# Two fused pairs of weights in group 9, background work in that group's first half, five heads under way, and another order of the pairs in the first output group

## The chip, the cores and the metric

The kernel runs on one core of one Trainium2 chip. The metric is the device time of one execution in microseconds (us), the median of several runs. TensorE is PE below, VectorE DVE, ScalarE ACT, GpSimd POOL and SyncE SP; PEld is the weight load of PE.

## The reference

One layer of an encoder works on x of 256 rows and 4096 columns, everything in float32:

```python
xn = rms_norm(x, norm_g)
h = einsum('bsd,de->bse', xn, w_in)                # 4096 x 14336
c_val, c_glu, c_gate, q, k, v, a_gate = split(h)   # seven parts of 2048 columns
conv_out = conformer_conv(c_val, c_glu, ...) * silu(c_gate)
q, k = rms_norm(q), rms_norm(k)                    # by head: 16 heads of 128
attn_out = longnet_mixture(q, k, v, rel_bias) * silu(a_gate)
y = x + einsum('bse,ed->bsd', concatenate([conv_out, attn_out]), w_out)   # 4096 x 4096
```

`conformer_conv` multiplies the value by a sigmoid gate, convolves every channel with 31 taps, normalises over the 2048 channels (LN below) and applies swish. `longnet_mixture` gives each head three patterns of dilated attention windows, combined by their softmax denominators.

## The kernel before

**Groups and pairs.** The two projections are 18 groups of 1024 output columns. Groups 0 to 3 give the convolution's value and GLU gate, 4 and 5 its gate, 6, 7, 9 and 11 queries and keys of four heads each (qk0 to qk3), 8, 10, 12 and 13 value and gate of four heads each (agv0 to agv3), and 14 to 17 are the output projection. A group runs over 4096 rows of weights in 16 steps, its slots; what a slot works on is a *pair*: two blocks of 128 rows, 256 x 1024 weights, 1 MB, loaded by SP (L252) into one of three `raw` buffers. Pairs are numbered through by u = 16 x group + slot, so `raw152` belongs to slot 8 of group 9. The next load into a buffer is issued when the last step of the pair that held it has been written.

**Plain and fused pairs.** Each float32 operand is split into a high and a low part, so that a product takes three fast matmuls (high x high, high x low, low x high). A *plain* pair costs ACT two casts (L1131, `wh`), DVE one subtraction (L1137, `wl`), and PE 24 matmuls of 512 columns (L1325, L1327). A *fused* pair is taken as a 2 x 2 block product with seven multiplications in place of eight, so PE runs 21 matmuls (L1192 to L1194, L1296, L1298); its weights need sums first: three subtractions L1155, the sums L1163, L1175, L1176 and the subtraction L1174 on DVE, and four casts on ACT (L1154, L1170). Four of its sums (m1, m5, m6, m7) gather in four more PSUM banks and are added to the group's result after the group's last fused pair, in the next plain pair (`add_more`: one copy by ACT, L1359, the rest on DVE, for the output groups L1363 to L1381). `FUSED` names the pairs that are fused: seven in most of groups 1 to 8, none in 9 to 13, four in group 14, seven in 15 to 17. `ORDERS` is the order of the pairs within a group. In group 14 pairs 0 to 7 are the 16 heads' columns of `w_out`'s rows (two heads a pair), 8 to 15 the convolution's.

**Weights ahead.** PE, DVE and ACT each run their instructions in the order in which the program wrote them. `Stream.step` writes the making of weights a few steps ahead of PE's use of them, as far as buffers go: four `ws` tiles and up to four halves under the tag `c4`, which they share with convolution and gate tiles (`C4` in number).

**Background work.** Between the weights the program writes everything else, in lanes of generators to which `pump` gives time for each matmul written (`credit`): convolution taps, LN, gates, heads, and the splitting of the projection's input for the output groups. One tap is four multiply-adds on DVE (L628), or four products by ACT (L562) that are added to the sum by DVE (L619) where `state["taps"]` is true, and otherwise by a DMA that POOL issues with an addition (L581). `head_lane = Lane(4)` lets four heads be under way at once. A head makes its scores (`psc`, L802, a short run of float32 matmuls on PE between the weights), bias and softmax (L812 to L830), a turn through DRAM (DVE L836, POOL L454 to write and L461 to read back), the product with the values (`po`, L847, again on PE) and the sum L852. Scores and `po` use the second set of PSUM banks (`state["side"]`), which only slots 1 up to the group's first fused pair give them. `mix_split_gen` (L865 to L890) makes the high and low parts `mh` and `ml` (L880, L882) of gated convolution and attention columns, pair by pair in the order of `ORDERS[14]`, and for the pairs that any output group fuses the sums `ms` and `msp` (L377 to L390). A convolution block's columns are ready when `gated_gen` has multiplied them with the gate (L733), which it loads back by four POOL DMAs (`far_g`, L461), block after block. Other POOL DMAs of that place are the write and the reads of a head's turned weights (`turn_p..d`, `pr`) and those of an attention gate (`turn_ag..d`, `agv`).

Of the kernel before, what the change touches and what calls it, by code (L numbers as in the profile page):

```python
# [11 lines left out]
F32 = mybir.dt.float32  # L12
F32R = mybir.dt.float32r
# [4 lines left out]
P = 128  # L18
# [24 lines left out]
SETTLED = 3000  # L43

CP_MIN = 900
C4 = 16

X_LOAD = {0: 12, 1: 16, 3: 20, 5: 24, 6: 28}
X_SQUARE = {4: 4, 5: 0, 6: 8, 7: 12, 8: 16, 9: 20, 10: 24, 11: 28}
# [17 lines left out]
FUSED_IN = range(1, 9)  # L67
SUMS = (2, 4, 6, 8, 10, 12, 13)
FUSED = [SUMS if g in FUSED_IN else () for g in range(N_IN)]
FUSED[1], FUSED[2] = (6, 8, 12), SUMS[1:]  # L70
FUSED += [range(4)] + 3 * [range(7)]
ORDERS = N_IN * [range(16)]
ORDERS += [(8, 9, 10, 11, 12, 13, 14, 0, 15, 1, 4, 2, 5, 3, 6, 7)]
ORDERS += 3 * [(8, 9, 0, 10, 1, 11, 2, 12, 3, 13, 4, 14, 5, 6, 15, 7)]

W_SLOTS, W_MORE = 4, 4
# [61 lines left out]
def layer_kernel(  # L138
# [16 lines left out]
    state = {"side": "side", "taps": True, "held": 0}  # L155
    const = ctx.enter_context(tc.tile_pool(name="const", bufs=1))
    sb = ctx.enter_context(tc.tile_pool(name="sb", bufs=1))
    ps = ctx.enter_context(tc.tile_pool(name="ps", bufs=1, space=bass.MemoryType.PSUM))

    def t4(name):  # L160
        return sb.tile([P, 4, 256], F32, tag="c4", bufs=C4, name=name)

    def t2(name):
        return sb.tile([P, 512], F32, tag="t2", bufs=5, name=name)

    def h2(name):
        return t2(name).rearrange("p (a b) -> p a b", a=2)
# [201 lines left out]
    def block_sums(j, src_of, parts, out, name, small=False):  # L369


        a11, a21, a12, a22 = (by_block(src_of[2 * j + k])[:, s] for k in range(2) for s in range(2))
        t = t2(f"{name}_{j}")
        s1, s2, s3, s4 = (
            t[:, P * i : P * i + P].rearrange("p (a i) -> p a i", a=4) for i in range(4)
        )
        nc.vector.tensor_sub(s1, a21, a22)  # L377
        nc.vector.tensor_sub(s2, s1, a11)
        yield 580
        nc.vector.tensor_sub(s3, a11, a21)  # L380
        nc.vector.tensor_add(s4, a12, s2)
        yield 580
        if small:
            both = [sb.tile([P, 512], F32R, tag="toep", bufs=4, name=f"{name}p{j}{i}") for i in "hl"]
        else:
            both = sb.tile([P, 2, 512], F32R, tag="c4", bufs=C4, name=f"{name}p{j}")
            both = both[:, 0], both[:, 1]
        nc.scalar.copy(both[0], t)
        yield 0, 620
        nc.vector.tensor_sub(both[1], t, both[0].bitcast(F32))  # L390
        names = {f"s{i + 1}": [b[:, P * i : P * i + P] for b in both] for i in range(4)}
        names["a11"] = [m[2 * j][:, :P] for m in parts]
        names["a12"] = [m[2 * j + 1][:, :P] for m in parts]
        names["a22"] = [m[2 * j + 1][:, P:] for m in parts]
        out[j] = names
        yield 690
# [146 lines left out]
    taps, made = deque(), deque()  # L543
# [239 lines left out]
    def head_gen(hg, hh):  # L783
        h = 4 * hg + hh
        hs = slice(DH * hh, DH * hh + DH)
        while hg not in qk_ready:
            yield
        T = sb.tile([P, 512], F32, tag="toep", bufs=4, name=f"T{h}")
        nc.sync.dma_start(
            T[:, :384],  # L790
            bass.AP(
# [9 lines left out]
        for it in range(2):  # L801
# [7 lines left out]
        window = bass.AP(  # L809
            tensor=T.tensor, offset=T.offset + S - 1, ap=[T.ap[0], [P, 2], [-1, 256]]  # L810
        )
# [76 lines left out]
            elif j in FUSED[-1]:  # L888
                later.append(j)

    post_lane, head_lane, gate_lane, mix_lane = Lane(2, (0,)), Lane(4), Lane(1, ()), Lane(1)
    fetch_lane, ag_lane = Lane(1, (1,)), Lane(1, ())
    conv_lane, ln_lane, cp_lane = Lane(1, ()), Lane(1, (0,)), Lane(1, (1,))
    center_lane = Lane(1, (1,))
# [150 lines left out]
    class Stream:  # L1045
# [159 lines left out]
        def group(self, g):  # L1205
# [3 lines left out]
            last_group, into = g == NG - 1, groups[g][0] == "out"  # L1209
# [8 lines left out]
            firsts = [s for s, j in enumerate(ORDERS[g]) if j in FUSED[g]]  # L1218
            window = range(1, (firsts + [n_pairs - 3])[0])
            for slot, j in enumerate(ORDERS[g]):  # L1220
                u = g * n_pairs + slot
                state["side"] = tags[1] if slot in window and len(window) > 4 else None
                state["taps"] = not firsts
                if g == n_in - 1:
                    progress["in"] = 2 * slot
                self.more = W_MORE if firsts and slot + 2 >= firsts[0] else 0
# [287 lines left out]
```

## Time and profile before

| | |
|---|---|
| runs | 1561.62 us median of 3 (1560.17 to 1565.84) |
| profiled execution, its own time | 1561.59 us |
| its span | 1559.8 us |
| matmul records on PE | 6844 |
| group 9 (windows of the trace) | 759.52 to 850.02 us |
| group 13 | 1126.14 to 1220.73 us |
| group 14 | 1220.73 to 1308.59 us |

The span runs from the first to the last instruction recorded; the execution's own time has 1.79 us around it. A group's limits are the starts of its first matmul and of the next group's.

### The profile page before, as it was taken

The numbers are of one execution on the slowest core, as the hardware profiler recorded it, in microseconds if no ns is written. First come the engines' busy times: TensorE is split into PE (matmuls) and PEld (weight loads), VectorE is DVE, ScalarE is ACT, GpSimd is POOL, SyncE is SP. The second block draws the span as 40 slices with busy tenths as digits, with TensorE's granted clock in tenths as the row PEclk, the third lists the DMA queues.
The fourth block names the chain that finished last, engine by engine and source line by source line (L and its number), as shares of the span: only waits on it lengthen the run. The fifth ranks groups of instructions, "written<-read, shape, count | busy, mean of one in ns | idle before, by whom it ended". The sixth has DMA issues, their size and how long they took to land.

```text
span 1559.8 us, 18654 instructions
## 1 busy us (share of the span) xinstructions
PE 1554.2 (100%) x6844; PEld 1285.2 (82%) x6844; DVE 1350.8 (87%) x1449; ACT 1017.3 (65%) x1564; POOL 148.5 (10%) x222
## 2 busy tenths in 40 slices
PE   9999999999999999999999999999999999999998
PEld 8888888888888888888888888888888888888887
DVE  7898799989899888999897989886676798998988
ACT  7665556767676677677778887776657654555453
POOL 0000000101010100001120012010240200000000
PEclk9999999999999999999999999999999999999999
DMA  9556567969788887789695668665886866666663
GB/s 350 199 201 231 189 218 241 274 218 267 241 258 254 243 246 256 228 247 251 226 313 188 230 229 266 213 230 203 251 270 209 252 223 230 239 217 240 234 240 119
DMA packets 80828, 367.91 MB, mean 236 GB/s; under 512 B 9152, under 2 KB 31296, under 8 KB 44128
## 3 DMA queue, kind: packets, MB, share of 16 engines
q1 hardware_dynamic: 50336, 317.86, 57.9%
q0 software_dynamic: 30112, 48.58, 14.3%
q8 instruction: 53, 0.87, 0.2%
q14 instruction: 39, 0.32, 0.1%
q10 hardware_dynamic: 288, 0.28, 0.1%
HBM read 328.57 MB, written 18.91 MB: 223 GB/s over the span
## 4 chain that ended last, share of the span: by engine, by line
PE 94%; DVE 2%; DMA 1%; issue 1%; ACT 1%; DVEq 0%; SPq 0%; ACTq 0%
PE c L1325 40%; PE c L1327 20%; PE m L1296 6%; PE c L1341 4%; PE m L1298 3%; PE c L1296 2%; PE c L1193 2%; PE c L1194 2%; PE c L1192 2%; PE c L1343 2%; PE acc L1033 2%; PE acc L1034 2%; PE acc L1036 2%; DMA raw<-in_w_dram 1%; PE c L1298 1%
## 5 line engine op out<-in xcount | busy, mean ns | idle before, releaser
L1137 DVE TENSOR_TENSOR wl<-raw,wh 128x2048 fp32r<-128x2048 f32 x196 | 448.2, 2289 | 146.9 <-ACT wh L1131 140.3
L1131 ACT CAST wh<-raw 128x1024 fp32r<-128x1024 f32 x392 | 390.7, 1047 | 194.0 <-PE c L1327 124.0
L1325 PE MATMUL c<-wh,nh 128*128 128x512 f32 x1152 | 450.2, 391 | 0.0
L1327 PE MATMUL c<-wh,nl 128*128 128x512 f32 x1152 | 448.4, 389 | 0.0
L1154 ACT CAST t<-raw 128x1024 fp32r<-128x1024 f32 x152 | 160.1, 1053 | 250.3 <-DVE raw L1163 171.1
L1325 PE MATMUL c<-wl,nh 128*128 128x512 f32 x1152 | 287.7, 392 | 0.0
L1325 PEld LDWEIGHTS c<-wh,nh 128*128 128x128 f32 x1152 | 216.3, 188 | 45.2
L1327 PEld LDWEIGHTS c<-wh,nl 128*128 128x128 f32 x1152 | 216.3, 188 | 45.1
L1325 PEld LDWEIGHTS c<-wl,nh 128*128 128x128 f32 x1152 | 216.3, 188 | 44.9
L1155 DVE TENSOR_TENSOR t<-raw,t 128x1024 fp32r<-128x1024 f32 x152 | 185.5, 1222 | 3.7 <-ACT t L1154 0.4
L562 ACT ACTIVATE cp<-a,wT 128x241 f32<-128x241 f32 (+14 forms) x312 | 131.4, 491 | 1.0 <-DVE cT L619 1.0
L1325 PE MATMUL c<-wh,mh 128*128 128x512 f32 x280 | 109.1, 390 | 0.0
L1327 PE MATMUL c<-wh,ml 128*128 128x512 f32 x280 | 108.9, 389 | 0.0
L581 POOL DMA_DIRECT2D cT<-cp x38 | 48.8, 1285 | 533.7 <-ACT cp L562 488.7
L1163 DVE TENSOR_TENSOR raw<-raw 128x1024 f32<-128x1024 f32 x76 | 93.1, 1225 | 2.6
L1155 DVE TENSOR_TENSOR b<-raw,b 128x1024 fp32r<-128x1024 f32 x76 | 92.7, 1220 | 1.6 <-ACT b L1154 1.0
L1154 ACT CAST b<-raw 128x1024 fp32r<-128x1024 f32 x76 | 79.6, 1047 | 3.5 <-PE c L1327 1.8
L1296 PE MATMUL m<-t,xsp 128*128 128x512 f32 x216 | 72.3, 389 | 0.0
L628 DVE SCALAR_TENSOR_TENSOR cT<-a,wT,cT 128x255 f32<-128x255 f32 (+8 forms) x168 | 68.9, 476 | 0.6
L1325 PE MATMUL c<-wl,mh 128*128 128x512 f32 x280 | 69.2, 389 | 0.0
L1327 PEld LDWEIGHTS c<-wh,ml 128*128 128x128 f32 x280 | 52.6, 188 | 10.9
L1325 PEld LDWEIGHTS c<-wl,mh 128*128 128x128 f32 x280 | 52.6, 188 | 10.9
(346 smaller groups left out, 2311.0 us busy)
## 6 DMA issues: line engine op xcount, KB each, us to landing
raw<-in_w_dram SPq DMA_DIRECT2D x286, 1024.0 KB, 5.0
xr<-in_x_dram SPq DMA_DIRECT2D x8, 512.0 KB, 6.5
out_dram<-xr SPq DMA_DIRECT2D x15, 256.0 KB, 7.5
xT<-in_x_cols_dram SPq DMA_DIRECT2D x7, 512.0 KB, 9.0
T<-bias_dram SPq DMA_DIRECT2D x16, 192.0 KB, 6.1
cT<-cp POOLq DMA_DIRECT2D x4, 488.0 KB, 6.7
cT<-cp POOLq DMA_DIRECT2D x4, 486.0 KB, 6.7
cT<-cp POOLq DMA_DIRECT2D x4, 484.0 KB, 6.1
```

Of the source, the lines that this page charges most:

```text
L562: nc.scalar.activation(cp[:, t, lo:hi], a[:, t, lo + sh : hi + sh], AF.Copy, scale=wT[:, 4 * cb + t, k : k + 1],)
L628: nc.vector.scalar_tensor_tensor(c[:, t, lo:hi], a[:, t, lo + sh : hi + sh], wT[:, 4 * cb + t, k : k + 1], c[:, t, lo:hi], op0=ALU.mult, o ...
L1131: nc.scalar.copy(h, raw_tiles[u][:, k])
L1137: nc.vector.tensor_sub(l, src, h.bitcast(F32))
L1154: nc.scalar.copy(h, src)
L1155: nc.vector.tensor_sub(l, src, h.bitcast(F32))
L1163: nc.vector.tensor_add(r[:, 0:4:3, :], r[:, 0:3:2, :], twice(r[:, 3, :]))
L1296: nc.tensor.matmul(acc, ah, b, start=begin, stop=end)
L1298: nc.tensor.matmul(acc, al, b, start=False, stop=False)
L1325: nc.tensor.matmul(acc, a[s][0], b[e], start=begin, stop=False)
L1327: nc.tensor.matmul(acc, a[s][1], b[e], start=False, stop=False)
L1341: nc.tensor.matmul(acc, a[s][0], b[e], start=False, stop=end)
```

## The change

The diff has five parts. `FUSED[9] = (8, 10)` makes the pairs in slots 8 and 10 of group 9 fused ones. `state["taps"]` says when DVE may add ACT's products; it was true in every slot of a group without fused pairs, and now also in slots 1 to 7 of group 9 (its `window`, up to the first fused pair), not after them. Scores, too, have their banks in that group in slots 1 to 7 only. `Lane(5)` lets a fifth head be under way, for which the turned weights `T` (tag `toep`) have five buffers instead of four and the tag `t2` six instead of five; `C4` gives up one tile for them. `ORDERS[14]` puts pairs 4 and 5 (heads 8 to 11) first, and its fused pairs 0 to 3 into slots 8, 10, 12 and 14, where they had slots 7, 9, 11 and 13; behind the last fused pair now stands one plain pair instead of two.

Counted over the whole program, the order has 6 matmuls of 512 columns fewer on PE, the two fused pairs' ones. The short runs of float32 matmuls (scores, `po` and LN's means) that stand between the weights' matmuls of groups 9 to 14 are 25 before and 17 after, with as many matmuls in them. DVE's tap multiply-adds (L628, four to a tap) go from 40 to 42 taps, its additions L619 from 40 to 37, and POOL's adding DMAs L581 from 38 to 39.

```diff
@@ -43,7 +43,7 @@
 SETTLED = 3000
 
 CP_MIN = 900
-C4 = 16
+C4 = 15
 
 X_LOAD = {0: 12, 1: 16, 3: 20, 5: 24, 6: 28}
 X_SQUARE = {4: 4, 5: 0, 6: 8, 7: 12, 8: 16, 9: 20, 10: 24, 11: 28}
@@ -67,10 +67,10 @@
 FUSED_IN = range(1, 9)
 SUMS = (2, 4, 6, 8, 10, 12, 13)
 FUSED = [SUMS if g in FUSED_IN else () for g in range(N_IN)]
-FUSED[1], FUSED[2] = (6, 8, 12), SUMS[1:]
+FUSED[1], FUSED[2], FUSED[9] = (6, 8, 12), SUMS[1:], (8, 10)
 FUSED += [range(4)] + 3 * [range(7)]
 ORDERS = N_IN * [range(16)]
-ORDERS += [(8, 9, 10, 11, 12, 13, 14, 0, 15, 1, 4, 2, 5, 3, 6, 7)]
+ORDERS += [(4, 5, 8, 9, 10, 11, 12, 13, 0, 14, 1, 15, 2, 6, 3, 7)]
 ORDERS += 3 * [(8, 9, 0, 10, 1, 11, 2, 12, 3, 13, 4, 14, 5, 6, 15, 7)]
 
 W_SLOTS, W_MORE = 4, 4
@@ -161,7 +161,7 @@
         return sb.tile([P, 4, 256], F32, tag="c4", bufs=C4, name=name)
 
     def t2(name):
-        return sb.tile([P, 512], F32, tag="t2", bufs=5, name=name)
+        return sb.tile([P, 512], F32, tag="t2", bufs=6, name=name)
 
     def h2(name):
         return t2(name).rearrange("p (a b) -> p a b", a=2)
@@ -381,7 +381,7 @@
         nc.vector.tensor_add(s4, a12, s2)
         yield 580
         if small:
-            both = [sb.tile([P, 512], F32R, tag="toep", bufs=4, name=f"{name}p{j}{i}") for i in "hl"]
+            both = [sb.tile([P, 512], F32R, tag="toep", bufs=5, name=f"{name}p{j}{i}") for i in "hl"]
         else:
             both = sb.tile([P, 2, 512], F32R, tag="c4", bufs=C4, name=f"{name}p{j}")
             both = both[:, 0], both[:, 1]
@@ -785,7 +785,7 @@
         hs = slice(DH * hh, DH * hh + DH)
         while hg not in qk_ready:
             yield
-        T = sb.tile([P, 512], F32, tag="toep", bufs=4, name=f"T{h}")
+        T = sb.tile([P, 512], F32, tag="toep", bufs=5, name=f"T{h}")
         nc.sync.dma_start(
             T[:, :384],
             bass.AP(
@@ -888,7 +888,7 @@
             elif j in FUSED[-1]:
                 later.append(j)
 
-    post_lane, head_lane, gate_lane, mix_lane = Lane(2, (0,)), Lane(4), Lane(1, ()), Lane(1)
+    post_lane, head_lane, gate_lane, mix_lane = Lane(2, (0,)), Lane(5), Lane(1, ()), Lane(1)
     fetch_lane, ag_lane = Lane(1, (1,)), Lane(1, ())
     conv_lane, ln_lane, cp_lane = Lane(1, ()), Lane(1, (0,)), Lane(1, (1,))
     center_lane = Lane(1, (1,))
@@ -1220,7 +1220,7 @@
             for slot, j in enumerate(ORDERS[g]):
                 u = g * n_pairs + slot
                 state["side"] = tags[1] if slot in window and len(window) > 4 else None
-                state["taps"] = not firsts
+                state["taps"] = not firsts or not into and len(window) > 4 and slot in window and g > FUSED_IN[1]
                 if g == n_in - 1:
                     progress["in"] = 2 * slot
                 self.more = W_MORE if firsts and slot + 2 >= firsts[0] else 0
```

**DVE in the middle of group 9.** Names: `wl151` is the low part of the plain pair in slot 7, `wl153` that of slot 9; `cT1` is a convolution sum, `cp` a product of ACT. Before:

```order
L1137 TENSOR_TENSOR wl151_6161<-raw151_6021,wh151_6144 128x2048
L628 SCALAR_TENSOR_TENSOR cT1_4342<-a1_4284,wT_72,cT1_4342 128x252 x4
L619 TENSOR_TENSOR cT1_4342<-cT1_4342,cp1_77 128x4x247
L1137 TENSOR_TENSOR wl152_6205<-raw152_6064,wh152_6193 128x2048
L628 SCALAR_TENSOR_TENSOR cT1_4342<-a1_4284,wT_72,cT1_4342 128x252 x4
L628 SCALAR_TENSOR_TENSOR cT1_4342<-a1_4284,wT_72,cT1_4342 128x251 x4
L1137 TENSOR_TENSOR wl153_6258<-raw153_6119,wh153_6241 128x2048
```

After:

```order
L1137 TENSOR_TENSOR wl151_6161<-raw151_6024,wh151_6144 128x2048
L1155 TENSOR_TENSOR b_1521_6166<-raw152_6062,b_1520_6165 128x1024
L1163 TENSOR_TENSOR raw152_6062<-raw152_6062 128x2x512
L1174 TENSOR_TENSOR b22_152_6170<-raw152_6062,b22_152_6170 128x512
L1175 TENSOR_TENSOR raw152_6062<-raw152_6062 128x512
L1176 TENSOR_TENSOR raw152_6062<-raw152_6062 128x512
L1155 TENSOR_TENSOR t13_152_6197<-raw152_6062,t13_152_6197 128x1024
L1155 TENSOR_TENSOR t42_152_6208<-raw152_6062,t42_152_6208 128x1024
L619 TENSOR_TENSOR cT1_4342<-cT1_4342,cp1_77 128x4x247
L1137 TENSOR_TENSOR wl153_6249<-raw153_6119,wh153_6229 128x2048
```

The pair of slot 8 has seven instructions for its sums and splits instead of one, and two taps' multiply-adds have left this place.

**POOL around the start of group 14.** Names as above; the number behind `far_g`, `turn_g` and `pr` is that of the convolution block or the head. Before:

```order
L461 DMA far_g1_9183<-turn_g1d0_3511 32x4x256 x4
L461 DMA far_g2_9285<-turn_g2d0_4126 32x4x256 x4
L461 DMA far_g3_9369<-turn_g3d0_4128 32x4x256 x4
L454 DMA turn_p12d0_9498<-T12_9104 128x512
L454 DMA turn_p13d0_9513<-T13_9106 128x512
L454 DMA turn_p14d0_9515<-T14_9108 128x512
L454 DMA turn_ag3d0_9598<-turn_ag30_9560 128x1024
L461 DMA pr12_9214<-turn_p12d0_9498 32x4x128 x4
L461 DMA pr13_9219<-turn_p13d0_9513 32x4x128 x4
L461 DMA pr14_9244<-turn_p14d0_9515 32x4x128 x4
L461 DMA agv3_0_9532<-turn_ag3d0_9598 32x4x256 x4
```

After:

```order
L454 DMA turn_p14d0_9501<-T14_9127 128x512
L454 DMA turn_p15d0_9503<-T15_9129 128x512
L461 DMA far_g1_9545<-turn_g1d0_3511 32x4x256 x4
L454 DMA turn_ag3d0_9605<-turn_ag30_9569 128x1024
L461 DMA pr13_9214<-turn_p13d0_9499 32x4x128 x4
L461 DMA pr14_9219<-turn_p14d0_9501 32x4x128 x4
L461 DMA pr15_9246<-turn_p15d0_9503 32x4x128 x4
L461 DMA far_g2_9664<-turn_g2d0_4126 32x4x256 x4
L461 DMA agv3_0_9536<-turn_ag3d0_9605 32x4x256 x4
L461 DMA far_g3_9762<-turn_g3d0_4128 32x4x256 x4
```

The gates of the convolution's blocks 2 and 3 were loaded ahead of the last heads' turns; now `far_g2` stands behind the write of `turn_ag3` and the reads of three heads.

**DVE in slots 2 to 5 of group 14,** which waits for one of these loads. Names: `wl227` to `wl229` are low parts of plain pairs, `ms_4` sums of the columns of heads 8 and 9, `ml12` and `ml13` low parts of the convolution's block 2, `wl219` to `wl221` the low parts of group 13's slots 11 to 13, `z` and `pr` tiles of the heads' softmax. Before:

```order
L1137 TENSOR_TENSOR wl219_9307<-raw219_9164,wh219_9296 128x2048
L882 TENSOR_TENSOR ml8_9201<-cT0_1472,mh8_9200 128x512
L1137 TENSOR_TENSOR wl220_9348<-raw220_9226,wh220_9337 128x2048
L733 TENSOR_TENSOR cT2_6415<-cT2_6415,far_g2_9285 128x1024
L826 RECIPROCAL z12_9217<-z12_9217 128x2
L826 RECIPROCAL z13_9222<-z13_9222 128x2
L826 RECIPROCAL z14_9247<-z14_9247 128x2
L812 SCALAR_TENSOR_TENSOR pr15_9377<-psc15_9328,T15_9260 128x512
L816 TENSOR_REDUCE nm15_9379<-pr15_9377 128x2
L1137 TENSOR_TENSOR wl221_9395<-raw221_9266,wh221_9382 128x2048
```

After:

```order
L377 TENSOR_TENSOR ms_4_9719<-agv2_0_8817 128x128
L378 TENSOR_TENSOR ms_4_9719<-ms_4_9719,agv2_0_8817 128x128
L380 TENSOR_TENSOR ms_4_9719<-agv2_0_8817 128x128
L381 TENSOR_TENSOR ms_4_9719<-agv2_0_8817,ms_4_9719 128x128
L1137 TENSOR_TENSOR wl228_9737<-raw228_9582,wh228_9722 128x2048
L733 TENSOR_TENSOR cT2_6565<-cT2_6565,far_g2_9664 128x1024
L390 TENSOR_TENSOR msp4_9735<-ms_4_9719,msp4_9735 128x512
L882 TENSOR_TENSOR ml12_9752<-cT2_6565,mh12_9751 128x512
L882 TENSOR_TENSOR ml13_9769<-cT2_6565,mh13_9768 128x512
L377 TENSOR_TENSOR ms_5_9784<-agv2_0_8817 128x128
L378 TENSOR_TENSOR ms_5_9784<-ms_5_9784,agv2_0_8817 128x128
L1137 TENSOR_TENSOR wl229_9787<-raw229_9641,wh229_9771 128x2048
```

The product with `far_g2` stood ahead of the low part of group 13's slot 13, and now stands between those of slots 4 and 5 of group 14.

**ACT at the end of group 14.** Names: `wh239` is the high part of the group's last pair, `wh240` and `wh241` those of group 15's first two, `m1s14` the copy of m1 with which `add_more` begins. Before:

```order
L1154 CAST t42_237_10099<-raw237_9993 128x1024
L1131 CAST wh238_10120<-raw238_10032 128x1024 x2
L1131 CAST wh239_10154<-raw239_10063 128x1024 x2
L1359 COPY m1s14_10172<-m1_14_9917 128x512
L1131 CAST wh240_10187<-raw240_10102 128x1024 x2
L1131 CAST wh241_10242<-raw241_10133 128x1024 x2
L1154 CAST b_2420_10249<-raw242_10161 128x1024
```

After:

```order
L1154 CAST t42_238_10154<-raw238_10048 128x1024
L1131 CAST wh239_10175<-raw239_10087 128x1024 x2
L1131 CAST wh240_10209<-raw240_10118 128x1024 x2
L1359 COPY m1s14_10215<-m1_14_9972 128x512
L1131 CAST wh241_10266<-raw241_10157 128x1024 x2
L1154 CAST b_2420_10273<-raw242_10188 128x1024
L1170 CAST b22_242_10278<-raw242_10188 128x512
```

The copy stood ahead of the casts for pair 240, and now stands behind them.

## The prediction

> **What bounds the kernel now.** I read the busy times first, then the chain of work that ended last, then PE's waits, then the groups one by one as windows. The page's busy line, its row of granted clocks and its chain by engine:
>
> ```profile
> PE 1554.2 (100%) x6844; PEld 1285.2 (82%) x6844; DVE 1350.8 (87%) x1449; ACT 1017.3 (65%) x1564; POOL 148.5 (10%) x222
> ...
> PEclk9999999999999999999999999999999999999999
> ...
> PE 94%; DVE 2%; DMA 1%; issue 1%; ACT 1%; DVEq 0%; SPq 0%; ACTq 0%
> ```
>
> PE is busy throughout, at full clock, and 94% of the chain is PE's own work. The view of waits has two rows for PE, and the first stands at the program's start:
>
> ```profile
> PE spin L1399 <- DVE ones L174: 1.1, 1, 1.1
> PE m L1296 <- ACT t L1154: 0.5, 1, 0.5
> ```
>
> So PE waits for data once, 0.5 us, in group 7. Whatever the change does elsewhere, time is gained only by giving PE fewer matmuls, and lost only where weights, sums or banks come later than PE wants them. Nothing can be gained from DVE, which is busy 87%, unless PE's work shrinks with it. The windows, one for each group from 8 to 15 (the columns are the stretch and its length, then busy time and instructions of PE, PEld, DVE, ACT and POOL, the clock, DMA's share and GB/s):
>
> ```profile
> core 0: us, PE busy (x) PEld busy (x) DVE busy (x) ACT busy (x) POOL busy (x), PEclk, DMA share, GB/s
> 676.98:759.52 82.54, 82.54 (x364) 68.13 (x363) 73.73 (x71) 63.04 (x112) 7.69 (x6) 1.00 0.81 241
> 759.52:850.02 90.50, 90.50 (x401) 75.13 (x400) 81.12 (x104) 70.10 (x131) 16.06 (x29) 1.00 0.81 256
> 850.02:938.88 88.86, 88.86 (x393) 73.61 (x392) 78.13 (x104) 72.76 (x153) 10.46 (x19) 1.00 0.62 213
> 938.88:1031.38 92.50, 92.50 (x409) 76.62 (x408) 82.10 (x100) 67.02 (x122) 16.56 (x30) 1.00 0.74 245
> 1031.38:1126.14 94.76, 94.76 (x419) 78.52 (x418) 67.43 (x70) 61.17 (x118) 15.95 (x29) 1.00 0.68 225
> 1126.14:1220.73 94.59, 94.59 (x419) 78.53 (x418) 67.90 (x72) 65.85 (x101) 19.27 (x35) 1.00 0.76 240
> 1220.73:1308.59 87.86, 87.86 (x389) 72.86 (x388) 74.07 (x88) 46.44 (x58) 12.07 (x22) 1.00 0.69 231
> 1308.59:1390.87 82.28, 82.28 (x364) 68.13 (x363) 76.70 (x74) 43.09 (x48) 0.00 (x0) 1.00 0.65 231
> ```
>
> PE is busy for the whole of each. Group 15 has nine plain and seven fused pairs, 9 x 24 + 7 x 21 = 363 matmuls in 82.28 us: 0.2267 us for one. An unfused group of 384 takes 87.04; group 9 has 3.46 more for eight float32 score instructions in one run, group 12 7.72 more for 17 in nine runs. Two unknowns, two equations: 0.426 us an instruction and 0.0535 for each run. Group 11 (12 in six runs) then comes to 5.43 over, where 5.46 stands in its row.
>
> **The change, part by part.**
>
> *Two fused pairs in group 9.* 2 x 3 matmuls x 0.2267 = **-1.36 us** on PE, if the weights are there in time. The DVE groups that make weights:
>
> ```profile
> L1137 DVE TENSOR_TENSOR wl<-raw,wh 128x2048 fp32r<-128x2048 f32 x196 | 448.2, 2289 | 146.9 <-ACT wh L1131 140.3
> L1155 DVE TENSOR_TENSOR t<-raw,t 128x1024 fp32r<-128x1024 f32 x152 | 185.5, 1222 | 3.7 <-ACT t L1154 0.4
> L1163 DVE TENSOR_TENSOR raw<-raw 128x1024 f32<-128x1024 f32 x76 | 93.1, 1225 | 2.6
> L1155 DVE TENSOR_TENSOR b<-raw,b 128x1024 fp32r<-128x1024 f32 x76 | 92.7, 1220 | 1.6 <-ACT b L1154 1.0
> L1175 DVE TENSOR_TENSOR raw<-raw 128x512 f32<-128x512 f32 x76 | 52.6, 692 | 2.6
> L1176 DVE TENSOR_TENSOR raw<-raw 128x512 f32<-128x512 f32 x76 | 52.6, 692 | 2.6
> L1174 DVE TENSOR_TENSOR b<-raw,b 128x512 fp32r<-128x512 f32 x76 | 52.0, 684 | 0.0
> ```
>
> A fused pair costs DVE 3 x 1.22 + 1.23 + 0.68 + 2 x 0.69 = 6.96 us against 2.29, for 4.76 us of PE: two of them add 9.3 us. Another 5.4 come from eight sums of 512 columns at about 0.68 (four of `add_more`, four of the result, which ACT copied before). Put on top of 81.12 in a group of some 86 to 90 us that wouldn't fit. It fits because the program moves taps and scores out: with these rows' durations, all that it writes for DVE between group 9's weights is 86 us after, 90 before (the place in the program and in time differ by a few us). The taps go to groups 10 to 13, where DVE has 10 to 27 us free in each of the rows above. Groups with seven fused pairs keep PE full at 73.73 of 82.54, so I cost this at nothing, hidden under DVE's idle time. If that cover went, each late pair would show whole on PE.
>
> *Fewer float32 runs.* The same scores, `po` and means stand in 17 runs instead of 25: 8 x 0.0535 = **-0.43 us**. The bounds are 0 and -0.6 (eight times 0.08, the same difference taken from group 14: eight instructions in two runs, 3.54 over its 372 matmuls, against group 9's 3.46).
>
> *Fifth head, buffers, C4.* These move heads earlier and remove no work of PE's. `C4`'s lost tile is one of 16; PE feels it only if weights run dry, which is rival D.
>
> *The start of group 14.* Start = G, 1220.73 before. Three gate products L733 and their low parts now fall into this group. By the order and the row durations, DVE has 39.5 us to do for slots 2 to 8 (35.0 before), while PE takes 7 x 5.44 + 3.46 (the `po` run, 8 x 0.426 + 0.05) - 0.68 = 40.9. So DVE has 1.4 us to spare in this stretch, where it could idle for 6 before. The load that it waits for stands on POOL behind two things:
>
> ```profile
> 1227.42 0.54 POOL L454 DMA_DIRECT2D turn_ag3d<-turn_ag  x1 [10.75 <-DVE turn_ag L487]
> 1228.17 2.22 POOL L461 DMA_DIRECT2D pr<-turn_p12d  x4 [0.21 <-ACT wh L1131]
> ...
> far_g<-turn_g2d POOLq DMA_DIRECT2D x4, 128.0 KB, 8.0
> ...
> pr<-turn_p3d POOLq DMA_DIRECT2D x4, 64.0 KB, 11.8
> ...
> 1241.12 2.28 DVE L1137 TENSOR_TENSOR wl<-raw,wh 128x2048 fp32r<-128x2048 f32 x1
> ...
> L733 DVE TENSOR_TENSOR cT<-cT,far_g 128x1024 f32<-128x1024 f32 x4 | 4.9, 1219 | 0.0
> L880 ACT CAST mh<-cT 128x512 fp32r<-128x512 f32 x8 | 4.9, 612 | 1.6 <-DVE cT L733 1.6
> L882 DVE TENSOR_TENSOR ml<-cT,mh 128x512 fp32r<-128x512 f32 x8 | 5.5, 685 | 3.9 <-ACT mh L880 3.9
> ```
>
> POOL waits for DVE's turn of the gate until G + 6.7. After it come, in the new order, that write (0.54), twelve `pr` reads (2.22 for four, so 6.7) and then the four of `far_g2` (2.2), the last issued at about G + 16.2. Landing takes 8.0 us by its own row: G + 22.3 for the first, 24.2 for the last. `wl228` ended at G + 22.7 before (1241.12 + 2.28); with another product and its low parts ahead of it I put it at G + 23.5, where DVE reaches the product and stands for 0.7 us. Behind the product (1.22) come two casts on ACT (2 x 0.61) and `wh229` (2.0): done at about G + 28.7, wanted at 30.7 (five slots of 5.44 and the `po` run). On DVE, three operations of about 0.69, two short sums (0.3 each) and `wl229` (2.28) come behind it: done at about G + 30.7, wanted 16 matmuls after `wh229`, at 34.3. So the wait itself is hidden, with 2 to 3 us in hand. What is late next are the fused pairs of slots 8 and 10, for which the 1.4 us of slack are already half used: I take **+0.4 us** of waits on PE there. The bounds: 0, as in before, and 3.0 with the longest landing (rival B).
>
> *The end of group 14.* ACT's copy of m1 now stands behind the casts for pair 240. The rows of the hand-over before, ACT then DVE:
>
> ```profile
> 1297.70 2.00 ACT L1131 CAST wh<-raw 128x1024 fp32r<-128x1024 f32 x2 [3.75 <-PE m L1296]
> 1299.61 0.58 ACT L1359 COPY m1s<-m 128x512 f32<-128x512 f32 x1
> 1301.78 2.00 ACT L1131 CAST wh<-raw 128x1024 fp32r<-128x1024 f32 x2 [1.60 <-PE c L1327]
> ...
> 1301.95 1.28 DVE L1363 TENSOR_TENSOR xr<-xr,m 128x512 f32<-128x512 f32 x2
> 1303.14 0.68 DVE L1366 TENSOR_TENSOR us<-m1s,m 128x512 f32<-128x512 f32 x1
> 1306.27 0.68 DVE L1381 TENSOR_TENSOR xr<-xr,vs 128x512 f32<-128x512 f32 x1
> 1306.87 2.28 DVE L1137 TENSOR_TENSOR wl<-raw,wh 128x2048 fp32r<-128x2048 f32 x1
> ```
>
> The DVE chain from L1366 to the end of `wl240` lasts 6.0 us (1303.14 to 1309.15). Let E be the end of the last fused pair. The copy can follow two casts (2.0) and take 0.58, so L1366 starts near E + 2.6 and `wl240` ends near E + 8.6. PE has 24 matmuls of the last plain pair and 16 of the next before it wants it: 40 x 0.2267 = E + 9.07. It holds by 0.5 us; I cost it at nothing, bounds 0 and 2.0 (the two casts whole).
>
> **Sum.** -1.36 - 0.43 + 0.4 = -1.4 us against the profiled execution's own time of 1561.59 (its span 1559.8 and 1.79 around it): **1560.2 us**. The median of the runs before is 1561.62, the same to 0.03.
>
> **Rivals.**
>
> *B, the late gate (slower).* If `far_g2` lands as late as the longest row of that queue, 11.8 us instead of 8.0, DVE stands 3.8 us longer ahead of everything in its queue. It decides from about 8 us of landing on, where the 2 to 3 us in hand and the 1.4 begin to be used up: with 11.8 the fused pairs of slots 8 and 10 are about 3.0 us late, 1561.59 - 1.79 + 0.4 + 3.0 = 1563.2. For it speak a queue that lands between 3 and 12 us; against it that `far_g`'s own rows give 8. [...]
>
> *C, the hand-over.* If `wl240` comes after PE wants it, up to 2.0 us are lost once: 1560.2 to 1562.2, 1561.5 in the middle. Against it stands the 0.5 us in hand.
>
> *D, the background does not fit.* With a tile fewer and taps moved back, a group of 10 to 13 or the fused pairs of group 9 run out of weights pair after pair. It needs DVE to be short of its 10 us of idle time per group; ten pairs late by 1 us give 1570. The rows above leave DVE 78 to 82 of 89 to 92 us busy in groups 10 and 11, which speaks against it. Here a second page bears: "TensorE: Matmul & The Clock Gate", Part 1, says that PE's clock halves after an idle window of about 3.4 us; no run here shows such a gap (the clock row is full throughout), and only this rival could make one.
>
> *N, it saves nothing.* Every microsecond taken from PE is waited out elsewhere: 1561.6, a case of B and C together.
>
> **How the numbers follow.** Forecast 0.72 (1559.4 to 1561.4); B 0.11; C with N 0.10; D 0.06, the descriptor rule 0.01. A measurement of this kernel can tell 0.5%, 7.8 us, from no change. No case saves that: even the whole gain of 1.8 is 0.1%, so faster 0.01. Slower by more than 7.8 us is D and the rule, less the part of D that stays smaller: 0.05. The rest, 0.94, is the same. The range takes in B and the spread of the runs: 1558.6 to 1564.5.
>
> **What would show it.** Group 9's window at 90.5 - 1.4 - 3.4 (its scores moved on) with PE busy for all of it; group 14's `far_g2` product on DVE waiting about 1 us near G + 23; no PE wait row above 1 us; `wl240` done less than 1 us before PE's use. Wrong would be a wait row for PE at L1325 or L1296 of 2 us and more, in group 9 (D), behind `far_g2` (B) or at the first pair of group 15 (C).

## The result, and the profile after

The changed kernel takes 1577.26 us (median of 4 runs, 1575.49 to 1587.09) against 1560.89 of the kernel before: 1.0118 times as long, with an interval of 1.0103 to 1.0133. Forecast were 1560.2 us and a range to 1564.5. The profiled execution is the longest of the four, 1587.09 us, 25.5 more than the one before; a profile of a shorter run is among the experiments (e1_again).

The busy line, the clocks and the chain of the page of the changed kernel:

```profile
PE 1561.3 (98%) x6838; PEld 1287.5 (81%) x6838; DVE 1363.9 (86%) x1474; ACT 1011.3 (64%) x1554; POOL 149.9 (9%) x223
...
PEclk9999999999999999999999998999999999999999
...
PE 32%; DMA 3%; issue 2%; DVE 1%; ACT 1%; POOL 1%; DVEq 0%; ACTq 0%; POOLq 0%
```

PE has its six matmuls fewer, and yet DMA and POOL now stand in the chain that ended last (its shares sum to about 40%, since it could be followed back only to the middle of the span). Three of its longest pieces, in order of time (start, us, what):

```profile
949.30 9.91 DMA qk<-turn_qk2d
959.21 9.30 DMA pr<-turn_p2d
...
1259.19 8.09 DMA far_g<-turn_g2d
```

Three loads by POOL. Who waits for them is in the view of PE's waits (engine, line, what it waited for, us in total, times, longest):

```profile
PE po L847 <- DMA pr<-turn_p2d: 8.8, 1, 8.8
PE c L1325 <- ACT wh L1131: 3.8, 3, 1.5
PE po L847 <- DMA pr<-turn_p11d: 3.5, 1, 3.5
PE m L1296 <- DVE agv L852: 2.3, 1, 2.3
```

Before, PE waited for data once, 0.5 us. Now two heads' products with the values, `po`, stand at the load of their turned weights, and three casts come late. By groups (9 to 15, columns as in the prediction):

```profile
758.80:844.48 85.68, 85.68 (x379) 70.95 (x378) 78.66 (x98) 55.99 (x96) 15.20 (x26) 1.00 0.81 257
844.48:937.72 93.24, 91.74 (x405) 75.71 (x404) 79.98 (x107) 76.32 (x159) 7.03 (x13) 1.00 0.64 215
937.72:1044.58 106.86, 98.09 (x421) 80.89 (x420) 81.19 (x102) 68.51 (x125) 24.99 (x46) 0.95 0.70 223
1044.58:1136.90 92.32, 92.32 (x409) 76.63 (x408) 74.60 (x90) 67.31 (x140) 15.41 (x28) 1.00 0.67 222
1136.90:1238.56 101.66, 98.08 (x421) 80.63 (x420) 72.35 (x77) 60.02 (x89) 15.43 (x28) 0.97 0.69 221
1238.56:1334.13 95.57, 90.66 (x389) 73.53 (x388) 74.95 (x86) 49.92 (x65) 13.70 (x25) 0.98 0.68 216
1334.13:1416.41 82.28, 82.28 (x364) 68.13 (x363) 77.16 (x73) 42.79 (x48) 0.00 (x0) 1.00 0.65 230
```

Against the rows of before: group 9 is 4.8 us shorter (its scores are gone from it, and six matmuls), group 10 4.4 longer, group 11 14.4, group 12 2.4 shorter, group 13 7.1 longer, group 14 7.7. Together that is 26.3 us (the groups ahead of them are 0.7 shorter). Some of it is scores that moved from one group to the next (groups 10 and 11 have 12 records of PE more each); the rest is waiting. Group 15, behind all of it, is the same to 0.01. Group 9, where the fused pairs are, has PE busy throughout. The time is lost one to five groups later.

**Where the waits come from.** Scores of the first four heads on PE, before and after (timelines):

```profile
814.17 3.61 PE L802 MATMUL psc<-qk,near_q 128*128 128x256 f32 x16
```

```profile
855.62 3.61 PE L802 MATMUL psc<-qk,near_q 128*128 128x256 f32 x16
```

They stand 41 us later: the fused pairs hold the second set of PSUM banks from slot 8 of group 9 on, so the scores went from slot 9 to slot 1 of the next group. What follows on POOL, before (the number in brackets is the idle time ahead and what ended it):

```profile
872.07 0.57 POOL L454 DMA_DIRECT2D turn_p0d<-T  x1 [48.36 <-DVE T L836]
...
903.11 2.18 POOL L461 DMA_DIRECT2D pr<-turn_p1d  x4 [4.71 <-ACT cp L562]
...
916.26 2.21 POOL L461 DMA_DIRECT2D pr<-turn_p2d  x4 [6.32 <-ACT wh L1131]
945.63 0.56 POOL L454 DMA_DIRECT2D turn_ag1d<-turn_ag  x1 [27.16 <-DVE turn_ag L487]
```

and after:

```profile
902.92 0.56 POOL L454 DMA_DIRECT2D turn_p0d<-T  x1 [53.52 <-DVE T L836]
...
936.78 0.54 POOL L454 DMA_DIRECT2D turn_qk2d<-turn_qk  x1 [4.87 <-DVE turn_qk L487]
937.32 2.23 POOL L461 DMA_DIRECT2D pr<-turn_p1d  x4
939.54 0.56 POOL L454 DMA_DIRECT2D turn_p2d<-T  x1
946.29 0.56 POOL L454 DMA_DIRECT2D turn_ag1d<-turn_ag  x1 [6.18 <-DVE turn_ag L487]
947.09 3.85 POOL L461 DMA_DIRECT2D qk<-turn_qk2d  x7 [0.24 <-ACT cp L562]
953.29 0.55 POOL L461 DMA_DIRECT2D qk<-turn_qk2d  x1 [2.35 <-DMA turn_ag1d<-turn_ag]
953.93 1.09 POOL L461 DMA_DIRECT2D pr<-turn_p2d  x2
957.08 0.55 POOL L461 DMA_DIRECT2D pr<-turn_p2d  x1 [2.05 <-DMA qk<-turn_qk2d]
959.21 0.56 POOL L461 DMA_DIRECT2D pr<-turn_p2d  x1 [1.58 <-DMA qk<-turn_qk2d]
```

Before, the reads of heads 1 and 2 were issued in the quiet second half of group 10, the last of them 29 us ahead of the rush that begins with `turn_ag1` in group 11. After, those of head 2 meet it: POOL stands for the turned gate `turn_ag1`, then issues the eight reads of `qk2`, then stands for transfers under way, and the last read of head 2 is issued at 959.21. PE came to head 2's `po` at 959.87 (it starts at 968.64, behind a wait of 8.77). That `po` is written where the program's count says that the load has landed (8.5 us, and 2 for the queue, behind the read), and everything behind it on PE waits too. Two windows of the trace, the wait and what follows it:

```profile
959.20:968.20 9.00, 0.68 (x3) 0.21 (x2) 2.74 (x5) 6.91 (x13) 3.34 (x6) 0.79 1.02 329
968.20:974.50 6.30, 5.86 (x14) 4.67 (x15) 0.30 (x1) 0.00 (x0) 3.38 (x7) 0.50 0.52 124
```

The granted clock is 0.50 for the 6.3 us behind the wait, so PE does half its work there: some 3 us more. The prediction thought such a gap possible in rival D alone. The Trainium skill, "TensorE: Matmul & The Clock Gate", Part 1, says that an idle window of about 3.4 us halves the clock until PE has been busy for about as long. This trace agrees in the size of the window and not in the wait that it takes: its windows with a clock of 0.50 throughout are one, two and three times 3.41 us long (1295.45 to 1298.86, 1169.15 to 1175.98, 964.35 to 974.59), and the first of them follows a wait of only 2.3 us.

In group 14 DVE stood at the load of rival B:

```profile
1267.48 1.23 DVE L733 TENSOR_TENSOR cT<-cT,far_g 128x1024 f32<-128x1024 f32 x1 [6.20 <-DMA far_g<-turn_g2d]
```

PE's own waits in that group come to 4.9 us: casts of 1.2 and 1.1, a low part of 0.3, and the 2.3 of the view above at a fused pair. The prediction's sum of POOL's issue times left out that POOL pauses between reads. One such pause stood in the trace of before, just behind the rows that the prediction shows, and the changed kernel has the like (before, then after):

```profile
1234.32 0.55 POOL L461 DMA_DIRECT2D pr<-turn_p13d  x1 [2.31 <-DMA pr<-turn_p12d]
```

```profile
1252.52 0.55 POOL L461 DMA_DIRECT2D pr<-turn_p14d  x1 [2.33 <-DMA turn_ag3d<-turn_ag]
```

### The profile page after: what moved, and what is told of

It reads as the page before. It is cut to its first block, busy times and chain, and to the rows that moved or that the text cites. A ratio compares the mean times of both kernels' runs of the same rounds, so it can differ in the third digit from the quotient of the medians.

```text
span 1585.3 us, 18634 instructions
## 1 busy us (share of the span) xinstructions
PE 1561.3 (98%) x6838; PEld 1287.5 (81%) x6838; DVE 1363.9 (86%) x1474; ACT 1011.3 (64%) x1554; POOL 149.9 (9%) x223
## 3 DMA queue, kind: packets, MB, share of 16 engines
q0 software_dynamic: 30640, 49.09, 14.4%
## 5 line engine op out<-in xcount | busy, mean ns | idle before, releaser
L1137 DVE TENSOR_TENSOR wl<-raw,wh 128x2048 fp32r<-128x2048 f32 x194 | 443.6, 2289 | 154.1 <-ACT wh L1131 132.3
L1131 ACT CAST wh<-raw 128x1024 fp32r<-128x1024 f32 x388 | 386.7, 1047 | 195.8 <-PE c L1327 120.4
L1325 PE MATMUL c<-wh,nh 128*128 128x512 f32 x1136 | 443.8, 391 | 1.5 <-ACT wh L1131 1.5
L1327 PE MATMUL c<-wh,nl 128*128 128x512 f32 x1136 | 442.3, 389 | 0.0
L1154 ACT CAST t<-raw 128x1024 fp32r<-128x1024 f32 x156 | 164.3, 1053 | 257.9 <-DVE raw L1163 176.9
L1155 DVE TENSOR_TENSOR t<-raw,t 128x1024 fp32r<-128x1024 f32 x156 | 190.4, 1222 | 3.6
L562 ACT ACTIVATE cp<-a,wT 128x241 f32<-128x241 f32 (+14 forms) x304 | 127.7, 490 | 1.9 <-DVE cT L619 1.9
L581 POOL DMA_DIRECT2D cT<-cp x39 | 50.1, 1285 | 549.2 <-ACT cp L562 497.7
L1296 PE MATMUL m<-t,xsp 128*128 128x512 f32 x228 | 76.4, 389 | 0.0
L628 DVE SCALAR_TENSOR_TENSOR cT<-a,wT,cT 128x255 f32<-128x255 f32 (+7 forms) x176 | 72.0, 474 | 0.5
L1325 PEld LDWEIGHTS c<-wh,mh 128*128 128x128 f32 x280 | 52.8, 189 | 14.5 <-ACT wh L1131 3.6
```

The source lines that it names most:

```text
L562: nc.scalar.activation(cp[:, t, lo:hi], a[:, t, lo + sh : hi + sh], AF.Copy, scale=wT[:, 4 * cb + t, k : k + 1],)
L581: nc.gpsimd.dma_start(conv["sum"][:, :, lo:hi], cp[:, :, lo:hi], accum_op=ALU.add)
L628: nc.vector.scalar_tensor_tensor(c[:, t, lo:hi], a[:, t, lo + sh : hi + sh], wT[:, 4 * cb + t, k : k + 1], c[:, t, lo:hi], op0=ALU.mult, o ...
L1131: nc.scalar.copy(h, raw_tiles[u][:, k])
L1137: nc.vector.tensor_sub(l, src, h.bitcast(F32))
L1154: nc.scalar.copy(h, src)
```

## The experiments

Unless another is named, each is timed against the kernel before, whose median was 1560.7 to 1561.0 each time.

**The changed kernel again (e1_again).**

> The changed kernel as it is, once more, since its profiled execution (1587.09 us) was some 10 us longer than its other three. Theory 1, the late heads (PE stands at po because POOL read the turned weights back late, since group 9's fused half moved heads 0 to 3 into group 10): a PE wait of 3 to 9 us at po in group 11 stands in this profile too, and makes the greater part of the loss; 1575 to 1587. Theory 2, the new order of group 14 (the late gate): the waits that recur are those of group 14, some 5 to 8 us, and those at po come and go.

1581.06 us (1576.94 to 1589.93). The waits in its profile (1576.94 us):

```profile
PE po L847 <- DMA pr<-turn_p2d: 6.8, 1, 6.8
PE c L1325 <- ACT wh L1131: 2.6, 2, 1.4
PE m L1296 <- DVE agv L852: 2.3, 1, 2.3
```

Head 2's wait recurs, head 11's doesn't, group 14's do. Its group 11 is still the longest, 104 us.

**Group 9's part alone (e2_g9_alone), and all but group 9's part (e3_no_g9).** The first puts this into the kernel before:

```diff
-FUSED[1], FUSED[2] = (6, 8, 12), SUMS[1:]
+FUSED[1], FUSED[2], FUSED[9] = (6, 8, 12), SUMS[1:], (8, 10)
-state["taps"] = not firsts
+state["taps"] = not firsts or not into and len(window) > 4 and slot in window and g > FUSED_IN[1]
```

> Only group 9's part of the change: the two fused pairs and the rule for the taps; four heads, C4 16 and the old order of group 14. The scores of heads 0 to 3 move from slot 9 of group 9 to slot 1 of group 10 as in the changed kernel. Theory 1: PE waits at po in group 11, 4 to 12 us with the slow clock behind it: 1564 to 1573. Theory 2: no wait above 1 us, 1559 to 1560.5.

The second takes the same lines out of the changed kernel.

> The changed kernel without group 9's part: five heads, the buffers and the new order of group 14 stay, no pair of group 9 is fused and the taps follow the old rule. The scores of heads 0 to 3 are back in slot 9 of group 9. Theory 1: no wait at po in groups 10 to 13; 1560 to 1566 with whatever group 14 still costs. Theory 2: group 14's 5 to 8 us stay, and with them most of the loss, 1567 and more.

Alone: 1594.21 us (1.0221, 1.0204 to 1.0238), worse than the whole change and beyond either expectation. Its waits:

```profile
PE po L847 <- DMA pr<-turn_p13d: 12.3, 1, 12.3
PE po L847 <- DMA pr<-turn_p2d: 3.8, 1, 3.8
PE po L847 <- DMA pr<-turn_p15d: 3.2, 1, 3.2
```

Without it: 1564.12 us (1.0019, 1.0010 to 1.0028), with waits of 1.9 and 1.0 us at `po` of heads 3 and 4, where none was expected. So group 9's part makes the loss, and the other parts of the change soften it: with four heads and the old order the last heads run into group 14, where their last scores start at 1266 us (1193 in the changed kernel).

**The old order of group 14 (e4_old_order),** in the changed kernel, and **the new order alone (e6_order_alone),** in the kernel before:

```diff
-ORDERS += [(8, 9, 10, 11, 12, 13, 14, 0, 15, 1, 4, 2, 5, 3, 6, 7)]
+ORDERS += [(4, 5, 8, 9, 10, 11, 12, 13, 0, 14, 1, 15, 2, 6, 3, 7)]
```

> The changed kernel with the old order of group 14's pairs. Theory 1: the waits at po in groups 11 and 13 stay, those for the late gate in group 14 go: 1568 to 1580. Theory 2: the loss goes, 1560 to 1563.

> The kernel before with only the new order of group 14's pairs. The heads stand where they did. Both theories of the waits at po: none. If the new order costs by itself (the copy of m1 behind two casts, sums of heads 8 to 11 first), group 14 is longer by 1 to 5 us: 1562 to 1566; if group 14's loss in the changed kernel comes from the late heads and gates alone: 1560 to 1562.

1579.07 us with the old order: nothing returned, with waits at `po` of 5.1 and 2.9 us, and group 14 with others of its own. The order alone: 1561.6 (1.0005, 0.9993 to 1.0017), no difference that can be told, though its profile (1563.22 us) has a wait of 2.1 us at `po` of head 10, which neither theory expected. As the cause of the loss, theory 2 is out. Against e2, e4 has only the fifth head and its buffers more, and is 15 us shorter, with its last scores at 1184 us: it is the fifth head that softens the loss.

**Five heads alone (e7_five_heads_alone),** in the kernel before (parts of the lines; the one with `toep` stands for two):

```diff
-C4 = 16
+C4 = 15
-tag="t2", bufs=5
+tag="t2", bufs=6
-tag="toep", bufs=4
+tag="toep", bufs=5
-head_lane = Lane(4)
+head_lane = Lane(5)
```

> The kernel before with only the fifth head and its buffers (C4 15, t2 6, toep 5). Without group 9's part and with the new order of group 14 the waits at po were 1.9 and 1.0 us, at heads 3 and 4, and the time 3.3 us over the kernel before. Theory 1 with the fifth head as a second source of crowding on POOL: the same waits here, 1563 to 1565. If those came of the new order: 1560 to 1561.5.

1563.13 us (1.0014, 1.0002 to 1.0026), waits of 1.3 and 0.6 us at `po` of heads 3 and 4: a small loss of the same kind, 2 us. That it comes from the reads of one head more in the same queue is likely and not shown.

**The heads' turns on SP (e13_heads_on_sp).** In the changed kernel, `turn_p` and `pr` are issued by SP (the three helpers that issue them get the queue as an argument; the diff shows the call alone):

```diff
-        yield from through_dram([tmp], [pr], 128, f"turn_p{h}")
+        yield from through_dram([tmp], [pr], 128, f"turn_p{h}", nc.sync)
```

> The changed kernel with one difference: the writes and reads of the heads' turned weights (turn_p, pr) are issued by SP, among the loads of the projections' weights, and not by POOL. The instructions of PE, DVE and ACT stand in the same order as in the changed kernel. Theory 1 (the reads come late because POOL's queue stands: behind its wait for the turned gate, behind qk2's eight reads, behind the limit of DMAs under way): the PE waits at po shrink below 2 us in group 11, far_g2 is read earlier too since twelve reads ahead of it are gone; 1560 to 1567. Theory 3 (the heads' chain on DVE and ACT is late itself, the queue matters little): the waits stay within 2 us of the changed kernel's, 1575 to 1585.

1571.5 us (1568.66 to 1577.41), in between. Its profile, the longest run, has group 14 at 88.94 us instead of 95.57, so `far_g2` came in time once the reads were off POOL. But head 2 still waits, and a cast waits more:

```profile
PE po L847 <- DMA pr<-turn_p2d: 6.2, 1, 6.2
PE c L1325 <- ACT wh L1131: 6.1, 1, 6.1
```

The read of head 2 now stood on SP behind two loads of weights; a queue free of others wasn't tried. The second row is another load on POOL: ACT stands at a copy of the convolution's block (`a<-far_a`, L507) at the end of group 9, with the casts for group 10 behind it. The changed kernel has that wait too, 9.0 us on ACT and 1.5 on PE.

**`po` later (e8_po_later),** in the changed kernel, which shifts the line numbers behind L828 by one:

```diff
         yield from through_dram([tmp], [pr], 128, f"turn_p{h}")
+        yield from landing(0)
```

> The changed kernel with po written one landing time (8.5 us of the program's count) later behind the read of the turned weights. Theory 1: the wait at po of head 2, 7 to 9 us, shrinks by about 8.5, those at later heads too; what moves to later groups may crowd group 14; 1565 to 1575. Theory 3: the waits move with po and keep their length, 1575 to 1585.

1577.64 us, no gain (the time of theory 3), though no wait at `po` is left. In their place:

```profile
PE c L1326 <- ACT wh L1132: 10.7, 2, 6.4
```

PE now stands at casts that stand behind ACT's copies L507 of loads `far_a2` and `far_a3`, 13.8 and 11.2 us. So theory 1 was too narrow: `po` is one of several places, on PE, ACT and DVE, at which an engine that runs in order meets a POOL load.

**Longer times assumed for all of them (e17_long_landing),** in the changed kernel, and **shorter ones in the kernel before (e18_before_short_landing):**

```diff
-LANDING = 8500
-QUEUED = 2000
+LANDING = 12000
+QUEUED = 5000
```

and

```diff
-LANDING = 8500
+LANDING = 4000
```

> The changed kernel with longer times assumed for what goes through DRAM: LANDING 12000 instead of 8500 ns of the program's count, QUEUED 5000 instead of 2000. So every instruction that takes a turned or far block back (po on PE, the casts and copies L507 on ACT, the products L733 on DVE) is written later behind its read. Theory 1 in its wider form (all the waits are in-order engines standing at a POOL load that the program took for landed): the waits at po and at L507 shrink to under 2 us each, PE's excess in groups 9 to 11 from some 14 us to under 4; heads get later, so group 14 may lose up to 5; 1562 to 1570. Theory 3 (DVE or ACT late themselves): no gain, 1575 and more.

> The kernel before, nothing fused in group 9, with LANDING 4000 instead of 8500. Its loads land in 4 to 12 us, so the wider theory 1 expects what the change showed, without the change: PE waits at po (one to several of 1 to 6 us) and ACT or DVE standing at loads with PE behind; 1565 to 1585. If the loads are in time whatever the program assumes: 1560 to 1562.

e17 takes 1610.67 us, the longest of all. Groups 9 to 13 have no PE wait above 0.7 us, as the wider theory says, but what was late is now later still, and group 14 needs the result:

```profile
PE c L1325 <- ACT mh L880: 35.3, 4, 14.9
PE po L847 <- DMA pr<-turn_p12d: 3.4, 1, 3.4
```

Group 14 grew to 144.6 us. e18 takes 1570.62 us (1.0065, 1.0049 to 1.0082): with nothing fused the same kind of wait appears, 4.6 us at casts behind ACT's copies of loads. No wait at `po` came, which I had expected there.

**One fused pair (e19_one_pair),** the changed kernel with `FUSED[9] = (8,)`, and **the rule for the taps alone (e20_taps_half),** the kernel before with:

```diff
-state["taps"] = not firsts
+state["taps"] = not firsts and not (g == 9 and slot > 7)
```

> The changed kernel with one fused pair in group 9 (slot 8) instead of two: 6.96 - 2.29 = 4.7 us less for DVE in that group's second half, the same closing of the second banks at slot 8. If the closing of the banks and of the taps moves everything (form a): the loss stays, 1570 to 1585. If it is DVE's load by the fused pairs that makes the turns of qk1 late (form b): turn_qk1 is written some 5 us earlier, far_a2 with it, and the loss halves, 1563 to 1570.

> The kernel before with the rule for the taps alone: from slot 8 of group 9 on DVE may not add ACT's products (POOL's adding DMAs do), no pair is fused, and the scores of heads 0 to 3 stay in slot 9. If the move of the scores into group 10 is what matters: no PE wait above 2 us, 1560 to 1563. If the rule for the taps alone crowds POOL: waits at po or at L507 as in the changed kernel, 1568 and more.

One pair: 1577.12 us, all of the loss, with one wait of 10.7 us at `po` of head 2. The rule alone: 1560.34 (0.9996, 0.9986 to 1.0005), nothing.

**The banks reopened (e21_banks_reopened).** The changed kernel with one condition more; all fused work stays where it was:

```diff
-state["side"] = tags[1] if slot in window and len(window) > 4 else None
+state["side"] = tags[1] if (slot in window and len(window) > 4) or (g == 9 and 12 <= slot < 13) else None
```

> The changed kernel with one difference: in group 9 the second set of PSUM banks is given to scores again from slot 12 on, behind the fused pairs of slots 8 and 10 and their sums. The scores of heads 0 to 3 stand in slot 12 of group 9 (changed kernel: slot 1 of group 10; before: slot 9), all fused work on DVE stays. Form a, the closing of the banks: the waits at po in groups 11 and 13 and those of group 14 go for the most part, 1562 to 1568. Form b, DVE's work for the fused pairs: po waits of 5 us and more stay, 1573 and more.

1564.93 us (1.0021, 1.0012 to 1.0030): three quarters of the loss are gone. The first scores and the heads' turns of its trace:

```profile
827.71 3.61 PE L802 MATMUL psc<-qk,near_q 128*128 128x256 f32 x16
```

```profile
878.59 0.56 POOL L454 DMA_DIRECT2D turn_p0d<-T  x1 [31.13 <-DVE cT L628]
...
909.27 2.19 POOL L461 DMA_DIRECT2D pr<-turn_p2d  x4
943.54 0.56 POOL L454 DMA_DIRECT2D turn_ag1d<-turn_ag  x1 [32.07 <-DVE turn_ag L487]
```

The reads of head 2 are again 34 us ahead of `turn_ag1`. The longest PE wait left is 1.9 us, in group 14, and 0.6 at `po`. The rest, 4 us, is as large as what e3 and e7 lose without any fused pair (3.3 and 2.1), but it stands elsewhere: theirs at `po` in group 11, e21's in group 14, which lasts 93.1 us. Up to there e21 is ahead: the last matmul of group 13 (L1341) starts at 1218.6 us, and at 1220.8 in the kernel before. So PE's gain is there until group 14 takes more than that back.

**The same on the kernel before, other places (e22_pairs_4_6, e23_one_pair_reopened).** Four heads, the old order of group 14, and DVE's taps allowed in all of group 9 but around the fused pairs:

```diff
-FUSED[1], FUSED[2] = (6, 8, 12), SUMS[1:]
+FUSED[1], FUSED[2], FUSED[9] = (6, 8, 12), SUMS[1:], (4, 6)
-state["side"] = tags[1] if slot in window and len(window) > 4 else None
-state["taps"] = not firsts
+state["side"] = tags[1] if (slot in window and len(window) > 4) or (g == 9 and 8 <= slot < 13) else None
+state["taps"] = not firsts or g == 9 and slot not in range(3, 8)
```

These are e22's lines; in e23 they have `(8,)`, `10 <= slot < 13` and `range(7, 10)`.

> The kernel before (four heads, old order of group 14) with two fused pairs in group 9, at slots 4 and 6, the banks given to scores again from slot 8 on, and DVE's additions of taps allowed outside slots 3 to 7. The scores stand in slot 12. Form a: no PE wait above 2 us; six matmuls fewer are 1.4 us, so 1559 to 1561. Form b: 1565 and more.

> The kernel before with one fused pair in group 9, at slot 8, the banks open again from slot 10 on and DVE's additions of taps allowed outside slots 7 to 9. The scores stand in slot 10, one slot later than before. Form a: no PE wait above 2 us, 0.7 us gained: 1559.5 to 1561. Form b: half the loss, 1565 and more.

Form a missed in both: 1582.7 us (1.0141) and 1586.62 (1.0165), times of form b. Groups 9 to 12 are clean in both, and the last matmul of group 13 starts earlier than in the kernel before (1219.5 and 1219.2 us), in e22 in spite of one wait of 2.2 us in that group. The loss is in group 14 (e22 first, then e23):

```profile
PE po L847 <- DMA pr<-turn_p14d: 15.5, 1, 15.5
```

```profile
PE c L1325 <- ACT mh L880: 17.1, 4, 8.1
```

In e23 the convolution is what is late. Its last multiply-add of a tap and its last product with a gate on DVE, before:

```profile
1042.49 1.64 DVE L628 SCALAR_TENSOR_TENSOR cT<-a,wT,cT 128x249 f32<-128x249 f32 x4
...
1207.62 1.22 DVE L733 TENSOR_TENSOR cT<-cT,far_g 128x1024 f32<-128x1024 f32 x1
```

and in e23:

```profile
1094.57 1.64 DVE L628 SCALAR_TENSOR_TENSOR cT<-a,wT,cT 128x248 f32<-128x248 f32 x4
...
1275.99 1.22 DVE L733 TENSOR_TENSOR cT<-cT,far_g 128x1024 f32<-128x1024 f32 x1
```

52 us later at the last multiply-add, 68 at the gate, and group 14 by its old order begins with the convolution's columns. So open banks are needed and not enough: with four heads and the old order, something of the background comes late to group 14. That DVE's time for the fused pairs alone makes it late fits and isn't shown (in e2, with the same two pairs as the changed kernel, the last product with a gate starts at 1217 us, and it is the heads that are late). Whether the fifth head or the new order saves e21 from this wasn't tried.

**Banks reopened and heads on SP (e24_reopened_sp),** e21 and e13 together.

> The changed kernel with the banks reopened from slot 12 of group 9 on (1564.9 us) and, besides, the heads' turned weights written and read by SP instead of POOL. If the 4 us left are POOL's queue: no wait at po, far_g2 in time, 1559 to 1562. If they are DVE's and ACT's own lateness at group 14, or if the raw loads on SP suffer: 1564 and more.

1564.78 us, as e21: the wait at `po` is gone, but group 14 is as long (94.4 us), with 1.9 us at low parts (`ml`) that DVE makes. So the last 4 us are not the heads' reads on POOL.

## Why the prediction was wrong, step by step

- **Six matmuls fewer on PE: right.** Group 9 was to last 90.5 - 1.4 - 3.4 = 85.7 us with PE busy throughout; it lasted 85.68.
- **Fused pairs' DVE work "hidden under DVE's idle time": right for the weights of group 9, wrong as a cost of nothing.** None of them came late (the first of group 10 did, by 1.5 us). But the background that made room was not free to move: in the changed kernel DVE's last multiply-add of a tap starts at 1094 us instead of 1042, its last product with a gate at 1280 instead of 1208, its last sum of a head (L852) at 1294 instead of 1263. I compared sums of DVE's time by group, and asked of `far_g2` alone by when group 14 needs it. e21, with the heads back in place, still pays 5.2 us in group 14. (DVE's own taps go from 42 to 44: L628 has 168 records before and 176 after. The 40 and 42 that I counted are wrong.)
- **"Fifth head, buffers, C4. These move heads earlier": the step that failed.** The heads' first scores came 41 us later, as the order of the program and my own sentence on group 9's window ("its scores moved on") said. I followed their matmuls (the fewer runs) and not the DMAs that go with them: what stands ahead of them on POOL at the new place, and that PE, in order, stands at `po` for the last of them. No rival named `po` as a place of waiting. The sentence itself holds for the last heads (e4 against e2) and leaves out the first. e3, e19, e20 and e21 show that in the changed kernel the closed banks and the scores' move carry most of the loss; that they do it through POOL's queue is read from the traces, and e13 bears it out in part. e7 shows 2 us for the fifth head that I put at nothing.
- **The start of group 14: the place was right, as rival B's; cause and size were off.** DVE stood for `far_g2`, 6.2 us and not 0.7, until 28.9 us into the group. The landing wasn't long, 7.2 us in the median. POOL issued the last of the reads at 20.6 us into the group and not at 16.2, since it paused for transfers under way (2.33, 1.20 and 0.82 us). The prediction priced this at 3.0 us of waiting on PE and gave it a chance of 0.11; group 14 is 7.7 us longer, with late casts, one late sum and a slow clock. Not all of that is the gate's: in e4, with the old order and no wait for `far_g2`, group 14 still lasts 94.1 us. For the "descriptor rule" that has a chance of 0.01 in the prediction no run shows anything: POOL's issues took 0.55 us each as before, and what delayed them were the pauses.
- **The end of group 14: right.** No wait of PE stands at the first pair of group 15, which lasts 82.28 us as before, and the order alone cost nothing (e6).
- **The clock: wrong place.** I said that only rival D could let PE stand long enough to lose its clock. One late load did.
- **The price of fewer float32 runs** (-0.43) can't be told from these runs by itself.

What stays open: whether scores in group 10 without any fused pair would lose as much wasn't tried, so the closed banks are shown as necessary for most of the loss (e21), not as enough by themselves. What in the background makes group 14 5.2 us longer in e21, and some 20 us and more in e22 and e23, wasn't separated, and in e22 the cause of the late head 14 wasn't followed.

No version here beats the kernel before; e20, which fuses nothing more, equals it.

## What to carry to other kernels

When a change moves work, follow every instruction of it, its DMAs above all, to the queue where it now stands, and ask which in-order engine will meet the result. A fixed guess of when a load has landed holds only as long as the queue ahead of it stays as it was; when the order around it changes, check the distance between the issue of each such load and its first use. PE was 100% busy here because the loads had slack, and a change worth 1.4 us spent it.

## What the runs showed of the hardware that I had not expected

- Behind a wait of 8.8 us PE's granted clock was 0.50 for 6.3 us, so this late operand cost about a third more than its wait. Behind one of 3.5 us it was 0.50 for 5.5 us (1170.47 to 1175.98), some 2.7 us more, and behind one of 2.3 us for 3.4. Not every wait of this length does it: in e4, behind one of 2.9 us, the clock stayed at 1.00 (1163.84 to 1170.00). The runs of one kernel that meets such waits differ by 13 us (1576.94 to 1589.93, e1), where those of the kernel before that were timed beside them lie within 3.
- POOL pauses between issues for transfers that are still under way: single pauses of up to 2.4 us ahead of a read, ended by the landing of a transfer some places earlier (953 to 967 us in the changed kernel), besides 0.55 us for an issue. The kernel before has them too (2.31 us at 1234.32).
